# FFN activations turned in squares of 32 on VectorE and carried to their partitions through DRAM, instead of transposes on TensorE

## The chip, the cores and the metric

The kernel runs on one core of a Trainium2 chip. The metric is the device time of one execution in microseconds, the median of several runs. A core has five engines with queues of their own, which meet only at semaphores: TensorE (PE; its weight loads are listed as PEld), VectorE (DVE), ScalarE (ACT), GpSimd (POOL) and SyncE (SP). Here SP issues every DMA. SBUF and PSUM have 128 partitions; TensorE writes to PSUM only.

## The reference, cut to what matters

One layer of a diffusion transformer in float32: modulation, two kinds of attention, an output projection, a LayerNorm, and then the part that the change touches, a SwiGLU FFN with 256 tokens, width 2048 and hidden width 5632:

```python
def swiglu(u, w_gate, w_up, w_down):
    return (jax.nn.silu(u @ w_gate) * (u @ w_up)) @ w_down

x = layer_norm(DN_ALPHA * x + g2 * swiglu(modulate(x, sh2, sc2), w_gate[layer], w_up[layer], w_down[layer]),
               ln2_g[layer], ln2_b[layer])
```

## The kernel before

**Products.** Every float32 product is made of three matmuls. A matrix is split in a high part `hi` (rounded to the TensorE's fp32r type by a ScalarE cast) and a low part `lo` (the rest, a VectorE subtraction); `mm3` (lines 224 to 226) adds x_hi·w_hi, x_hi·w_lo and x_lo·w_hi into one PSUM bank.

**A step.** `load_split` loads 1 MB of a weight, 4 row tiles of 128 by 512 columns, with one DMA on SP (`load_raw`, line 194) into one of 4 `raw` buffers, and splits it in two halves of 128x1024 (`split_raw`, lines 214 and 215) into one of 4 `hi` and 4 `lo` buffers. `project` then runs 24 matmuls on it: 4 row tiles, 2 token tiles `t`, 3 products. So one half serves 12 matmuls, and the four halves in the buffers serve two steps. The order of a queue here is the order in which the tile framework's scheduler puts the instructions; only an earlier part of the kernel has its order written out by hand (`Flow`).

**The FFN.** The hidden width is cut into 11 blocks `f` of 512. For the first 10 blocks, one or two of the four row groups have been multiplied earlier and their sums kept in `spills[f]`, a pair of tiles for gate and up. The main loop over `f` does the remaining groups, first of `w_gate`, then of `w_up`: 3 + 3 steps for blocks 0 to 2, 2 + 2 for blocks 3 to 9, 4 + 4 for block 10. After the last step `activate` adds the kept sums (lines 1291 and 1292), applies silu on ScalarE (line 1295) and multiplies on VectorE (line 1297): `hh`, 128 tokens by 512 hidden columns, for each `t`.

**The flip.** The product with `w_down` sums over the hidden width, so hidden columns have to lie on partitions. `flip` transposes `hh` on TensorE, four transposes of 128x128 against an identity into one PSUM bank (line 1304), and `split` (lines 220 and 221) makes `hTh[f]` and `hTl[f]` of it. Flips wait in the list `flips` and are run after the first step of the next block. `hTh[f+1]` and `hTl[f+1]` lie in the memory of `spills[f]`.

**w_down.** Four column blocks `n` of 512 follow; each takes 11 steps, and step g needs `hTh[g]` and `hTl[g]`. Beside them VectorE sums the rows of the gate g2 from `w_ada` (line 332, 1 MB loads that share the `raw` buffers), and two loads of 1 MB bring ln2's rows. After each column block `residual` (lines 962 to 964) scales, adds and takes statistics; the last LayerNorm ends the kernel.

Of the kernel before, what the change touches and what calls it, by code (L numbers as in the profile page):

```python
# [12 lines left out]
F32 = mybir.dt.float32  # L13
# [4 lines left out]
AF = mybir.ActivationFunctionType  # L18
# [17 lines left out]
NB = 512  # L36
# [113 lines left out]
def dit_layer(ctx: ExitStack, tc: tile.TileContext, x, c, cx, c_ctx, w_ada, b_ada, w_in, q_norm_g,  # L150
              k_norm_g, sink_logit, w_out, ln1_g, ln1_b, w_gate, w_up, w_down, ln2_g, ln2_b,
              rope_cos, rope_sin, out):
    nc = tc.nc
    x, c, cx = x[0], c, cx[0]
# [11 lines left out]
    def wk_bank():  # L166
        return wk_ps.tile([P, NB], F32, tag="wk", name="wk")
# [51 lines left out]
    def split(hi, lo, src):  # L219
        nc.scalar.copy(hi, src)  # L220
        nc.vector.tensor_tensor(lo, src, hi.bitcast(F32), op=ALU.subtract)
# [184 lines left out]
    def t2k(name, shape=(P, NB), dtype=F32):  # L406
        return pa.tile(list(shape), dtype, tag="t2k", name=name, bufs=T2K)
# [551 lines left out]
    def residual(t, n, ps, gate, base, pool, bufs):  # L959
        y = pool.tile([P, NB], F32, tag="t2k", name="yt", bufs=bufs)  # L960
        sl = slice(n * NB, (n + 1) * NB)
        nc.vector.tensor_mul(y, ps, gate[:, sl])
        nc.vector.tensor_add(base[:, t, sl], base[:, t, sl], y)
        nc.vector.bn_stats(stats[:, t, n, :], base[:, t, sl])
# [205 lines left out]
    a = F.add("SP", 1000, ln_loads)  # L1170
    a = F.add("PE", 150, ln_flip, [(a, -SLACK)], [lroom])
# [4 lines left out]
    a = flow_vector((3 * D, 4 * D), NB, adav, (END - 14, END + 24))  # L1176
# [64 lines left out]
    a = F.add("DVE", 3300, lambda: scalars(0), [outs[n, 0] for n in range(4)])  # L1241
# [5 lines left out]
    ea.close()  # L1247


    pb = ctx.enter_context(tc.tile_pool(name="pb", bufs=1, reuse_waits="tile"))  # L1250
    u2h = pb.tile([P, KD, SEQ], F32R, tag="u2h", name="u2h")
    u2l = pb.tile([P, KD, SEQ], F32R, tag="u2l", name="u2l")
    hTh = [pb.tile([P, 4, SEQ], F32R, tag=f"hTh{f}", name="hTh") if f < KF // 4 - SPLIT_F else None for f in range(KF // 4)]
    hTl = [pb.tile([P, 4, SEQ], F32R, tag=f"hTl{f}", name="hTl") if f < KF // 4 - SPLIT_F else None for f in range(KF // 4)]

    def z_part(kk):
        ps = wk_bank()
        for j in range(2):
            for t in range(NT):
                nc.tensor.transpose(ps[:, (j * 2 + t) * P : (j * 2 + t + 1) * P],  # L1260
                                    xt[:, t, (kk + j) * P : (kk + j + 1) * P], ident)
        uf = pb.tile([P, 2, SEQ], F32, tag="t2k", name="uf2", bufs=3)
        for j in range(2):
            nc.scalar.activation(uf[:, j, :], ps[:, j * SEQ : (j + 1) * SEQ], AF.Identity,
                                 bias=mB[:, kk + j : kk + j + 1], scale=mA[:, kk + j : kk + j + 1])
        nc.scalar.copy(u2h[:, kk : kk + 2, :], uf)
        nc.vector.tensor_tensor(u2l[:, kk : kk + 2, :], uf, u2h[:, kk : kk + 2, :].bitcast(F32), op=ALU.subtract)
# [16 lines left out]
            for t in range(NT):  # L1284
                mm3(accs[t], u2h[:, k, t * P : (t + 1) * P], u2l[:, k, t * P : (t + 1) * P], w[j], k == first, k == last)

    def activate(f, t, gate, up, spill):

        if spill is not None:
            sg, su = spill[0][:, t, :], spill[1][:, t, :]  # L1290
            nc.vector.tensor_add(sg, sg, gate)
            nc.vector.tensor_add(su, su, up)
# [4 lines left out]
        nc.vector.tensor_mul(hh, up, sl)
        return hh

    def flip(f, t, hh):  # L1300

        ps = wk_bank()
        for j in range(4):
            nc.tensor.transpose(ps[:, j * P : (j + 1) * P], hh[:, j * P : (j + 1) * P], ident)  # L1304
        if hTh[f] is None:
            hTh[f] = pb.tile([P, 4, SEQ], F32R, tag=f"hTh{f}", name="hTh")
            hTl[f] = pb.tile([P, 4, SEQ], F32R, tag=f"hTl{f}", name="hTl")
        split(hTh[f][:, :, t * P : (t + 1) * P], hTl[f][:, :, t * P : (t + 1) * P], ps.rearrange("p (j q) -> p j q", j=4))

# [3 lines left out]
    spills, first_half = [], []  # L1313
# [18 lines left out]
    def z_rest(t, kk):  # L1332

        ps = zbanks[t, kk]
        tt = slice(t * P, (t + 1) * P)
        uf = pb.tile([P, 2, SEQ], F32, tag="t2k", name="uf2", bufs=3)[:, :, :P]
        for j in range(2):
            nc.scalar.activation(uf[:, j, :], ps[:, j * P : (j + 1) * P], AF.Identity,
                                 bias=mB[:, kk + j : kk + j + 1], scale=mA[:, kk + j : kk + j + 1])
        nc.scalar.copy(u2h[:, kk : kk + 2, tt], uf)  # L1340
        nc.vector.tensor_tensor(u2l[:, kk : kk + 2, tt], uf, u2h[:, kk : kk + 2, tt].bitcast(F32), op=ALU.subtract)  # L1341
# [39 lines left out]
        z_part(kk)  # L1381
    run(first_half[cutoff:])
    flips = []
    for f in range(FFN // NB):
        if 5 <= f < 9:
            residual_base(f - 5)
        gu = []
        for w_ in (w_gate, w_up):
            accs = [acc_bank() for _ in range(NT)]
            g0 = groups[f]  # L1390
            for g in range(g0, ng):
                project(accs, w_, f, g, g0 * 4, KD - 1)
# [3 lines left out]
        for t in range(NT):
            hh = activate(f, t, gu[0][t], gu[1][t], spills[f] if f < SPLIT_F else None)
            flips.append(lambda f=f, t=t, hh=hh: flip(f, t, hh))
    while flips:
        flips.pop(0)()  # L1400
# [97 lines left out]
```

## Time and profile before

| | |
|---|---|
| three runs | 1173.62 us median (1171.78 to 1175.6) |
| the profiled execution | 1172.63 us; span from first to last instruction 1170.9 us |
| mean granted TensorE clock | 0.995 |
| TensorE matmul busy / weight loads | 1144.9 us / 928.6 us |
| VectorE / ScalarE / GpSimd busy | 822.3 / 537.5 / 25.5 us |
| DMA | 292.95 MB, mean 250 GB/s |
| FFN main loop, from block 0's first step to block 10's last | about 611 to 911 us of the span |
| w_down | about 911 to 1150 us |

Times in the views are microseconds from the start of the span. A row of the timeline reads: start, duration, engine, line, operation, out<-in, shape, count, and in brackets how long the engine was idle before and what ended that. A row of the groups reads: line, engine, operation, shapes, count | busy us, mean ns of one | idle time before. Matmuls overlap in the pipeline, so the distance between their starts counts, not their length.

### The profile page before, as it was taken

How to read it: one execution, taken by the hardware profiler on the slowest of the kernel's cores; microseconds unless marked ns; L12 is line 12 of the kernel's file. 1: busy time of each engine (PE TensorE's matmuls, PEld its weight loads, DVE VectorE, ACT ScalarE, POOL GpSimd, SP SyncE). 2: the span in 40 equal slices, each digit the busy share in tenths (PEclk: the TensorE clock that was granted, in tenths of full speed). 3: DMA queues.
4: the chain of work that ended last, by engine and by line, in shares of the span. 5: the costliest groups of instructions: out<-in, count | busy, mean ns of one | idle time of the engine just before them, and what ended most of it. 6: DMA issues, size and time to landing. Idle time of an engine off the chain costs nothing.

```text
span 1170.9 us, 14367 instructions
## 1 busy us (share of the span) xinstructions
PE 1144.9 (98%) x5563; PEld 928.6 (79%) x5563; DVE 822.3 (70%) x1064; ACT 537.5 (46%) x760; POOL 25.5 (2%) x44
## 2 busy tenths in 40 slices
PE   8999999999999989999999999999999999999995
PEld 8767588888887778888888888888888788888884
DVE  4763588888899887766767566665665777676556
ACT  3341542777776255545454444444444433433440
POOL 1000030000000000000000000000000000000000
PEclk9999999999999999999999999999999999999997
DMA  8999988526587678889957555555556898877531
GB/s 266 390 403 397 357 360 287 181 72 215 182 290 280 225 271 320 302 293 316 322 194 239 182 189 196 188 180 180 184 198 212 299 330 317 283 257 256 192 132 73
DMA packets 150716, 292.95 MB, mean 250 GB/s; under 512 B 5580, under 2 KB 20332, under 8 KB 148343
## 3 DMA queue, kind: packets, MB, share of 16 engines
q1 hardware_dynamic: 150648, 292.04, 71.4%
q8 instruction: 44, 0.72, 0.2%
q14 instruction: 24, 0.20, 0.0%
HBM read 289.92 MB, written 2.10 MB: 249 GB/s over the span
## 4 chain that ended last, share of the span: by engine, by line
PE 93%; DVE 4%; DMA 2%; ACT 1%; issue 0%; SPq 0%; DVEq 0%; ACTq 0%
PE acc L224 27%; PE acc L225 27%; PE acc L226 27%; PE wk L865 2%; PE wk L485 2%; PE acc L1070 1%; PE wk L854 1%; PE wk L1304 1%; PE wk L224 1%; PE wk L226 1%; PE wk L225 1%; PE wk L342 1%; DMA lgb<-in_ln_b_dram 1%; PE wk L572 1%; DVE adav L332 1%; DVE lo L215 0%
## 5 line engine op out<-in xcount | busy, mean ns | idle before, releaser
L215 DVE TENSOR_TENSOR lo<-raw,hi 128x1024 fp32r<-128x1024 f32 x258 | 313.8, 1223 | 206.0 <-ACT hi L214 202.6
L214 ACT CAST hi<-raw 128x1024 fp32r<-128x1024 f32 x258 | 271.1, 1055 | 353.0 <-PE acc L226 331.3
L224 PE MATMUL acc<-hi,u2h 128*128 128x512 f32 x704 | 275.5, 391 | 1.2 <-ACT u2h L1340 1.2
L225 PE MATMUL acc<-lo,u2h 128*128 128x512 f32 x704 | 274.2, 389 | 0.8 <-DVE lo L215 0.8
L226 PE MATMUL acc<-hi,u2l 128*128 128x512 f32 x704 | 274.1, 389 | 0.0
L225 PEld LDWEIGHTS acc<-lo,u2h 128*128 128x128 f32 x704 | 132.2, 188 | 28.4 <-DVE lo L215 1.6
L224 PEld LDWEIGHTS acc<-hi,u2h 128*128 128x128 f32 x704 | 132.2, 188 | 28.2 <-ACT u2h L1340 1.4
L226 PEld LDWEIGHTS acc<-hi,u2l 128*128 128x128 f32 x704 | 132.2, 188 | 27.7 <-DVE u2l L1341 0.2
L446 ACT CAST hi<-raw 128x1024 fp32r<-128x1024 f32 (+1 forms) x86 | 87.9, 1033 | 135.3 <-PE acc L226 68.9
L224 PE MATMUL acc<-hi,hTh 128*128 128x512 f32 x344 | 135.5, 394 | 0.0
L226 PE MATMUL acc<-hi,hTl 128*128 128x512 f32 x344 | 134.0, 390 | 0.0
L225 PE MATMUL acc<-lo,hTh 128*128 128x512 f32 x344 | 134.0, 389 | 0.0
L332 DVE SCALAR_TENSOR_TENSOR adav<-raw,cs,adav 128x512 f32<-128x512 f32 (+1 forms) x128 | 121.4, 948 | 9.0 <-DMA raw<-in_w_ada_dram 7.2
L449 DVE TENSOR_TENSOR lo<-raw,hi 128x1024 fp32r<-128x1024 f32 (+1 forms) x86 | 102.5, 1198 | 28.0 <-ACT hi L446 27.7
L224 PE MATMUL acc<-hi,uh 128*128 128x512 f32 x256 | 102.8, 402 | 1.0 <-ACT hi L446 1.0
L225 PE MATMUL acc<-lo,uh 128*128 128x512 f32 x256 | 100.2, 391 | 1.1 <-DVE lo L449 1.1
L226 PE MATMUL acc<-hi,ul 128*128 128x512 f32 x256 | 99.9, 390 | 0.0
L225 PEld LDWEIGHTS acc<-lo,hTh 128*128 128x128 f32 x344 | 64.6, 188 | 14.4 <-issue 1.0
L224 PEld LDWEIGHTS acc<-hi,hTh 128*128 128x128 f32 x344 | 64.6, 188 | 14.1 <-issue 1.0
L226 PEld LDWEIGHTS acc<-hi,hTl 128*128 128x128 f32 x344 | 64.6, 188 | 13.4
L224 PEld LDWEIGHTS acc<-hi,uh 128*128 128x128 f32 x256 | 48.1, 188 | 17.7 <-issue 4.6
L225 PEld LDWEIGHTS acc<-lo,uh 128*128 128x128 f32 x256 | 48.1, 188 | 11.0 <-DVE lo L449 2.0
(201 smaller groups left out, 1166.8 us busy)
## 6 DMA issues: line engine op xcount, KB each, us to landing
raw<-in_w_ada_dram SPq DMA_DIRECT2D x72, 1024.0 KB, 7.0
raw<-in_w_gate_dram SPq DMA_DIRECT2D x44, 1024.0 KB, 5.2
raw<-in_w_up_dram SPq DMA_DIRECT2D x44, 1024.0 KB, 5.1
raw<-in_w_down_dram SPq DMA_DIRECT2D x44, 1024.0 KB, 5.6
raw<-in_w_ada_dram SPq DMA_DIRECT2D x48, 512.0 KB, 4.9
raw<-in_w_in_dram SPq DMA_DIRECT2D x18, 1024.0 KB, 8.0
raw<-in_w_out_dram SPq DMA_DIRECT2D x16, 1024.0 KB, 4.9
raw<-in_w_in_dram SPq DMA_DIRECT2D x10, 512.0 KB, 8.2
```

The costliest lines, as they stand in the source:

```text
L214: nc.scalar.copy(hi[:, :n], raw[:, s : s + n])
L215: nc.vector.tensor_tensor(lo[:, :n], raw[:, s : s + n], hi[:, :n].bitcast(F32), op=ALU.subtract)
L224: nc.tensor.matmul(ps, lhsT=xh, rhs=w[0], start=first, stop=False)
L225: nc.tensor.matmul(ps, lhsT=xh, rhs=w[1], start=False, stop=False)
L226: nc.tensor.matmul(ps, lhsT=xl, rhs=w[0], start=False, stop=last)
L332: nc.vector.scalar_tensor_tensor(a[:, c : c + piece], raw[:, f : f + piece], cs[:, g * (G4 * NB // w) + j, 2:3], a[:, c : c + piece], op0= ...
L342: nc.tensor.matmul(ps, lhsT=ones, rhs=sb[:, s : s + NB], start=True, stop=True)
L446: nc.scalar.copy(hl.hi[:, :n], raw.t[:, s : s + n])
L449: nc.vector.tensor_tensor(hl.lo[:, :n], raw.t[:, s : s + n], hl.hi[:, :n].bitcast(F32), op=ALU.subtract)
L485: nc.tensor.matmul(bank.t[32 * j : 32 * j + 32, :width], lhsT=cs[:, k, 2 - 2 * i : 34 - 2 * i], rhs=raw.t[:, c * width : (c + 1) * width], ...
L572: nc.tensor.transpose(ps.t[:, (j * 2 + t) * P : (j * 2 + t + 1) * P], src, ident)
L865: nc.tensor.matmul(o_ps.t[:, : 2 * P], lhsT=v, rhs=pT.t[:, k].rearrange("p h q -> p (h q)"), start=k == 0, stop=k == 3)
```

## The change

The flip leaves TensorE and PSUM. `activate` writes its product in place (for blocks 0 to 9 in the gate half of the spill, for block 10 in a scratch buffer). `squares` turns each square of 32x32 within `hh` on VectorE, one instruction for a 128x512 tile: what stood on partition i of a group of 32 is now at column i, but the groups of 32 partitions are still in their old place. `put` writes the result to a tile in DRAM, one DMA for each group of 32 partitions, in runs of 128 values (512 B); `get` reads it back with rows of 512 values to the 128 partitions where the hidden columns belong. `place` then splits the SBUF tile into `hTh[f]` and `hTl[f]`, as before from PSUM. For each block that is 2 VectorE transposes, 8 puts of 64 KB and 2 gets of 256 KB, all on SP. The three parts are held back by `turn`, which counts steps: puts after 6 further steps in the order of the program, gets after 8, placing after 9. Two pools of small buffers grow from 3 to 4.

```diff
+PUT, GET, PLACE = 6, 8, 9
...
+    scratch = ctx.enter_context(tc.tile_pool(name="scratch", bufs=1, space=bass.MemoryType.DRAM))
...
-    def activate(f, t, gate, up, spill):
-
-        if spill is not None:
-            sg, su = spill[0][:, t, :], spill[1][:, t, :]
+    def activate(f, t, gate, up, hh):
+
+        if f < SPLIT_F:
+            sg, su = spills[f][0][:, t, :], spills[f][1][:, t, :]
             nc.vector.tensor_add(sg, sg, gate)
             nc.vector.tensor_add(su, su, up)
             gate, up = sg, su
-        sl = pb.tile([P, NB], F32, tag="t2k", name="sl", bufs=3)
-        nc.scalar.activation(sl, gate, AF.Silu)
-        hh = pb.tile([P, NB], F32, tag="t2k", name="hh", bufs=3)
-        nc.vector.tensor_mul(hh, up, sl)
-        return hh
-
-    def flip(f, t, hh):
-
-        ps = wk_bank()
-        for j in range(4):
-            nc.tensor.transpose(ps[:, j * P : (j + 1) * P], hh[:, j * P : (j + 1) * P], ident)
+        nc.scalar.activation(hh, gate, AF.Silu)
+        nc.vector.tensor_mul(hh, up, hh)
...
+    def squares(hh, hx):
+        nc.vector.transpose(hx.rearrange("p (r q i) -> p q r i", r=4, q=Q), hh.rearrange("p (q r i) -> p q r i", r=4, q=Q))
+
+    def put(hx):
+        hd = scratch.tile([4, 32, 4, P], F32, tag="hd", name="hd", bufs=4)
+        for a in range(4):
+            nc.sync.dma_start(hd[:, :, a, :].rearrange("r i x -> i r x"),
+                              hx[32 * a : 32 * a + 32, :].rearrange("i (r x) -> i r x", r=4))
+        return hd
+
+    def get(hd, hf):
+        nc.sync.dma_start(hf, hd.rearrange("r i a x -> (r i) (a x)"))
+
+    def place(f, t, hf):
+
         if hTh[f] is None:
             hTh[f] = pb.tile([P, 4, SEQ], F32R, tag=f"hTh{f}", name="hTh")
             hTl[f] = pb.tile([P, 4, SEQ], F32R, tag=f"hTl{f}", name="hTl")
-        split(hTh[f][:, :, t * P : (t + 1) * P], hTl[f][:, :, t * P : (t + 1) * P], ps.rearrange("p (j q) -> p j q", j=4))
+        hi, lo = (h[f][:, :, t * P : (t + 1) * P].rearrange("p q (a i) -> p q a i", a=4) for h in (hTh, hTl))
+        split(hi, lo, hf.rearrange("p (a q i) -> p q a i", a=4, q=Q))
+
+    def flip_steps(f, gu):
+
+        if f < SPLIT_F:
+            hh, hx = ([c[:, t, :] for t in range(NT)] for c in spills[f])
+        else:
+            hh, hx = ([t2k(name) for t in range(NT)] for name in ("hh", "hx"))
+        for t in range(NT):
+            activate(f, t, gu[0][t], gu[1][t], hh[t])
+            squares(hh[t], hx[t])
...
+        return [[PUT, puts], [GET, gets], [PLACE, places]]
...
+    def turn():
+
+        for e in flips:
+            e[0] -= 1
+        for e in [e for e in flips if e[0] <= 0]:
+            flips.remove(e)
+            e[1]()
+
...
             for g in range(g0, ng):
                 project(accs, w_, f, g, g0 * 4, KD - 1)
-                while flips:
-                    flips.pop(0)()
+                turn()
             gu.append(accs)
...
+        flips += flip_steps(f, gu)
...
             for t in range(NT):
                 mms(g * 4, w, t)
+            turn()
```

On TensorE the order changes only by the transposes that are gone: 8 behind the first step after each of the blocks 0 to 9, and 4 + 4 inside the first step of w_down for block 10. On the other engines the instructions move. (Line numbers of the changed kernel are higher: lo is L216, the cast hi L215, the split of the turned tile L221 and L222, the sums L1293 and L1294.)

VectorE from the gate sums of one of the blocks 3 to 9 to those of the next, before:

```order
L1291 TENSOR_TENSOR spill<-spill,acc 128x512 x2
L215 TENSOR_TENSOR lo<-raw,hi 128x1024 x4
L1292 TENSOR_TENSOR spill<-spill,acc 128x512 x2
L1297 TENSOR_TENSOR hh<-spill,sl 128x512
L215 TENSOR_TENSOR lo<-raw,hi 128x1024
L1297 TENSOR_TENSOR hh<-spill,sl 128x512
L215 TENSOR_TENSOR lo<-raw,hi 128x1024 x2
L221 TENSOR_TENSOR hTl<-wk,hTh 128x4x128 x2
L215 TENSOR_TENSOR lo<-raw,hi 128x1024
```

and now:

```order
L1293 TENSOR_TENSOR spill<-spill,acc 128x512 x2
L216 TENSOR_TENSOR lo<-raw,hi 128x1024 x4
L1294 TENSOR_TENSOR spill<-spill,acc 128x512 x2
L1297 TENSOR_TENSOR spill<-spill 128x512 x2
L1307 STREAM_TRANSPOSE spill<-spill 128x4x4x32 x2
L216 TENSOR_TENSOR lo<-raw,hi 128x1024 x2
L222 TENSOR_TENSOR hTl<-spill,hTh 128x4x128 x2
L216 TENSOR_TENSOR lo<-raw,hi 128x1024 x2
```

Both products and both transposes now stand in one run behind the up sums, with no lo between; the hTl after them belongs to the block before, not to this one.

ScalarE in the same stretch, from the silu of a block on, now:

```order
L1296 ACTIVATE spill<-spill 128x512 x2
L215 CAST hi<-raw 128x1024 x3
L221 CAST hTh<-spill 128x4x128
L215 CAST hi<-raw 128x1024
L221 CAST hTh<-spill 128x4x128
L215 CAST hi<-raw 128x1024 x4
```

The cast of a turned tile (of the block before) used to wait for TensorE; here its input `spill` is what the get has brought, and the fourth hi stands behind it.

SP between the loads of one block (the first gate load stands ahead of these rows), now, with the semaphores that each waits for (DVE, or one of the eight that the DMAs take in turn):

```order
L1312 DMA hd<-spill 32x4x128 [waits DVE_49]
L1312 DMA hd<-spill 32x4x128 x2
L195 DMA raw<-in_w_gate_dram 128x4x512 [waits DMAHW5_49,DVE_49]
L1312 DMA hd<-spill 32x4x128 [waits DMAHW6_49]
L1312 DMA hd<-spill 32x4x128 [waits DMAHW7_49]
L1312 DMA hd<-spill 32x4x128 [waits DMAHW0_49]
L1312 DMA hd<-spill 32x4x128 [waits DMAHW1_49]
L1312 DMA hd<-spill 32x4x128 [waits DMAHW2_49]
L195 DMA raw<-in_w_up_dram 128x4x512 [waits DMAHW3_49,DVE_49]
L195 DMA raw<-in_w_up_dram 128x4x512 [waits DMAHW4_49,DVE_49]
L1317 DMA spill<-hd 128x512 [waits DMAHW6_49,DMAHW5_49]
L1317 DMA spill<-hd 128x512 [waits DMAHW2_49,DMAHW7_49,DMAHW1_49,DMAHW0_49]
```

Before, these were four loads in a row, two of gate and two of up. The first put waits for the squares of the block that ended last. Three puts stand ahead of the second gate load and five behind it; the gets stand behind both up loads and wait for the puts.

More of the change, by code (lines that the diff above doesn't have):

```diff
@@ L1261, in z_part @@
                                     xt[:, t, (kk + j) * P : (kk + j + 1) * P], ident)
-        uf = pb.tile([P, 2, SEQ], F32, tag="t2k", name="uf2", bufs=3)
+        uf = pb.tile([P, 2, SEQ], F32, tag="t2k", name="uf2", bufs=4)
         for j in range(2):
@@ L1293, in activate, with t2k @@
             gate, up = sg, su
-        sl = pb.tile([P, NB], F32, tag="t2k", name="sl", bufs=3)
-        nc.scalar.activation(sl, gate, AF.Silu)
-        hh = pb.tile([P, NB], F32, tag="t2k", name="hh", bufs=3)
-        nc.vector.tensor_mul(hh, up, sl)
-        return hh
-    def flip(f, t, hh):
-        ps = wk_bank()
-        for j in range(4):
-            nc.tensor.transpose(ps[:, j * P : (j + 1) * P], hh[:, j * P : (j + 1) * P], ident)
+        nc.scalar.activation(hh, gate, AF.Silu)
+        nc.vector.tensor_mul(hh, up, hh)
+    Q = 4
+    def t2k(name):
+        return pb.tile([P, NB], F32, tag="t2k", name=name, bufs=4)
+    def squares(hh, hx):
[9 more added lines that the diff above has]
+    def place(f, t, hf):
         if hTh[f] is None:
@@ L1307, in flip, with puts, gets, places @@
             hTl[f] = pb.tile([P, 4, SEQ], F32R, tag=f"hTl{f}", name="hTl")
-        split(hTh[f][:, :, t * P : (t + 1) * P], hTl[f][:, :, t * P : (t + 1) * P], ps.rearrange("p (j q) -> p j q", j=4))
+        hi, lo = (h[f][:, :, t * P : (t + 1) * P].rearrange("p q (a i) -> p q a i", a=4) for h in (hTh, hTl))
[8 more added lines that the diff above has]
+            squares(hh[t], hx[t])
+        hd, hf = {}, {}
+        def puts():
+            for t in range(NT):
+                hd[t] = put(hx[t])
+        def gets():
+            for t in range(NT):
+                hf[t] = hh[t] if f < SPLIT_F else t2k("hf")
+                get(hd[t], hf[t])
+        def places():
+            for t in range(NT):
+                place(f, t, hf[t])
+        return [[PUT, puts], [GET, gets], [PLACE, places]]
     groups = [1 if f < ONE_F else EARLY_G if f < SPLIT_F else 0 for f in range(FFN // NB)]
@@ L1335, in z_rest @@
         tt = slice(t * P, (t + 1) * P)
-        uf = pb.tile([P, 2, SEQ], F32, tag="t2k", name="uf2", bufs=3)[:, :, :P]
+        uf = pb.tile([P, 2, SEQ], F32, tag="t2k", name="uf2", bufs=4)[:, :, :P]
         for j in range(2):
@@ L1392, in dit_layer @@
                 project(accs, w_, f, g, g0 * 4, KD - 1)
-                while flips:
-                    flips.pop(0)()
+                turn()
             gu.append(accs)
[L1396 to L1400, printed above, removed]
+        flips += flip_steps(f, gu)
     l2 = pb.tile([P, 2, D], F32, tag="u2l", name="l2")
@@ L1432, in tail @@
                     mms(g * 4, w, t)
-                residual(t, n, accs[t], g2sb, xt, pb, 3)
+                residual(t, n, accs[t], g2sb, xt, pb, 4)
         return [lambda g=g: step(g) for g in range(KF // G4 - together)] + [tail]
```

## The prediction

> **What bounds the kernel now.** I read the page first: which engine is full, and which the chain of waits runs over.
>
> ```profile
> span 1170.9 us, 14367 instructions
> ...
> PE 1144.9 (98%) x5563; PEld 928.6 (79%) x5563; DVE 822.3 (70%) x1064; ACT 537.5 (46%) x760; POOL 25.5 (2%) x44
> ...
> PE 93%; DVE 4%; DMA 2%; ACT 1%; issue 0%; SPq 0%; DVEq 0%; ACTq 0%
> ...
> raw<-in_w_up_dram SPq DMA_DIRECT2D x44, 1024.0 KB, 5.1
> ```
>
> TensorE sets the end: 93% of the chain. Work taken from it is gained one for one as long as nobody else makes it wait. Next come the windows, for the room elsewhere (us; busy time of PE, PEld, DVE, ACT, POOL; clock, DMA share, GB/s), and the waits.
>
> ```profile
> 5.00:14.00 9.00, 9.00 (x89) 8.68 (x88) 0.00 (x0) 0.57 (x1) 0.00 (x0) 1.00 0.99 310
> ...
> 737.00:895.00 158.00, 158.00 (x724) 131.44 (x723) 98.04 (x106) 72.18 (x83) 0.00 (x0) 1.00 0.57 186
> 915.00:970.00 55.00, 55.00 (x240) 44.83 (x239) 40.90 (x46) 21.68 (x23) 0.96 (x2) 1.00 0.91 328
> ...
> ACT hi L214 <- PE acc L226: 331.3, 211, 3.5
> ...
> SPq L194 <- DVE lo L215: 413.4, 100, 7.2
> ```
>
> From 737 to 895 (FFN blocks 4 to 10) PE never idles, VectorE is busy 62% and the DMA engines 57%. Casts wait for PE to free a hi/lo buffer, and loads wait for VectorE to free a raw buffer: everybody upstream is as far ahead as the buffers let them be. That is the cover for what the change adds.
>
> **What is removed.** The chain in order of time (start, us, what) and PE's timeline give the price of the flips.
>
> ```profile
> 736.43 0.87 PE wk L1304 x8
> 759.09 0.87 PE wk L1304 x8
> ...
> 758.47 0.39 PE L225 MATMUL acc<-lo,u2h 128*128 128x512 f32 x1
> 758.69 0.39 PE L226 MATMUL acc<-hi,u2l 128*128 128x512 f32 x1
> 758.93 1.03 PE L1304 MATMUL wk<-ident,hh 128*128 128x128 f32 x8
> 759.72 0.48 PE L224 MATMUL acc<-hi,u2h 128*128 128x512 f32 x1
> 760.03 0.40 PE L225 MATMUL acc<-lo,u2h 128*128 128x512 f32 x1
> 760.26 0.39 PE L226 MATMUL acc<-hi,u2l 128*128 128x512 f32 x1
> ...
> 911.84 0.39 PE L224 MATMUL acc<-hi,hTh 128*128 128x512 f32 x1
> 912.94 0.66 PE L1304 MATMUL wk<-ident,hh 128*128 128x128 f32 x4 [0.71 <-DVE hh L1297]
> 914.49 0.40 PE L224 MATMUL acc<-hi,hTh 128*128 128x512 f32 x1
> ```
>
> Matmuls start every 0.227 us. From 758.69 to 760.26 three starts take 1.57 instead of 0.68: eight transposes cost 0.89 us. The period says the same: 759.09 - 736.43 = 22.66, less 96 matmuls x 0.227 = 21.77. Ten blocks: 8.9 us. The last block's flips fall between 911.84 and 914.49: three starts take 2.65 instead of 0.68, so 1.97, its 0.71 wait for VectorE included. Removed from PE: **10.9 us**. PE gets nothing in return.
>
> **VectorE and ScalarE.** Groups and timeline:
>
> ```profile
> L221 DVE TENSOR_TENSOR hTl<-wk,hTh 128x512 fp32r<-128x512 f32 x22 | 14.1, 682 | 0.0
> ...
> L588 DVE TENSOR_TENSOR ul<-uf,uh 128x512 fp32r<-128x512 f32 x14 | 9.8, 731 | 5.7 <-ACT uh L585 5.6
> ...
> L585 ACT CAST uh<-uf 128x512 fp32r<-128x512 f32 x14 | 8.3, 641 | 0.1
> ...
> 774.74 1.23 DVE L215 TENSOR_TENSOR lo<-raw,hi 128x1024 fp32r<-128x1024 f32 x1 [1.49 <-ACT hi L214]
> 775.89 1.28 DVE L1292 TENSOR_TENSOR spill<-spill,acc 128x512 f32<-128x512 f32 x2
> 777.08 0.69 DVE L1297 TENSOR_TENSOR hh<-spill,sl 128x512 f32<-128x512 f32 x1
> ...
> 775.91 0.39 PE L226 MATMUL acc<-hi,u2l 128*128 128x512 f32 x1
> ...
> 779.05 1.05 ACT L214 CAST hi<-raw 128x1024 fp32r<-128x1024 f32 x1 [1.14 <-PE acc L226]
> ```
>
> The split of the turned tile now reads SBUF instead of PSUM, and the row of such a split (L588) is 0.05 us longer: nothing, since VectorE is not the bound. New are 22 square transposes, 128x512 f32, which no row shows. All VectorE rows of that size lie near 0.7 us; I take 0.7, from 0.5 (a gain on no path) to 2.0 (three passes). Where they matter: let T be the end of a block's last matmul, which starts at 775.91, so T = 776.1. In the new order (shown with the change) VectorE does the up sums 1.28, both products 1.38 and both transposes 1.4 in one run, where a lo stood between the products before. It starts some 0.2 after T, is free at T+4.2, and the next lo is ready at T+5.4. Four lo stand between gate sums and up sums, and of the four hi/lo buffers only the one of the last half step is still in use at T. So three halves lie ready for PE, 12 matmuls or 2.72 us each, and PE needs the next lo at T+8.2. That covers the run by 2.8 us. With no halves in store the whole run would stand on PE's path, and the 1.4 of the transposes would cost 15 us over 11 blocks.
>
> The skill gives a price of its own: in the Trainium skill, VectorE: DVE Perf Modes, "The three transpose paths", 128x128 bf16 takes 311 ns on VectorE; four of them would be an estimated 1.2 us, and the sum would stay the same. No run so far shows it.
>
> **SP and the DMA trip.** SP's timeline (start, us from first to last issue):
>
> ```profile
> 773.28 6.02 SPq L194 DMA_DIRECT2D raw<-in_w_gate_dram  x2
> 784.11 6.71 SPq L194 DMA_DIRECT2D raw<-in_w_up_dram  x2
> ...
> out_dram<-xt SPq DMA_DIRECT2D x8, 256.0 KB, 2.3
> ...
> raw<-in_w_ada_dram SPq DMA_DIRECT2D x2, 1024.0 KB, 7.9
> ```
>
> Against T = 776.1 the loads leave at -2.8, +2.8, +8.0 and +14.3. The pair of gate loads belongs to the next block but one, and SP takes its queue in order. Now three puts stand ahead of the second load and wait for the squares: they leave at T+4.2, the load at T+5.4 (2.6 late), five puts by T+7.5, and the up loads behind them on time. Per block SP issues ten more, about 0.4 us each: 4 of 21.8. A raw tile is cast three steps of 5.44 us after its issue, so 2.6 late plus 5.1 of landing is covered. The gets stand behind the second up load: T+14.7. Each put takes a semaphore of eight in turn, so the eighth waits until the first has landed. With a landing of L for a put and G for a get, the data are there at T + max(14.7, 4.2 + 2L) + G. ScalarE has that cast behind the third hi after the next block's gate sums; it can make this hi when the last step's first half frees its buffer, so it reaches the cast at T+21.8-2.7+1.1 = T+20.1. The hi behind it feeds the lo due at T+29.9 (a period of 21.77 after T+8.16), so PE notices only data later than T+27.0: 29.9 less lo 1.22, hi 1.05 and the cast itself 0.64. L and G are bounded by 2.3 (the 256 KB stores) and 7.9 (megabytes in pieces of 512 B, queued in pairs, the two ada loads above). I take 5.1, as behind one weight load: there at T+19.8, no wait. At 7.9: T+27.9, 0.9 a block. Traffic: 5 MB a block for 4 raises the share from 0.57 to 0.74 in the shorter period; pieces of 512 B ran at 310 GB/s with 0.99 busy, so they are about as cheap per byte as the 326 (186/0.57) of this stage; if each cost as much as a 2 KB piece, 1280 beside 2048, the share would be 0.96. Cost: nothing, up to 9 us.
>
> **First column block of w_down.** Block 10's puts and gets fall here, and its two splits come between gate-2 sums; the two loads of ln2 move out to later blocks.
>
> ```profile
> 972.29 0.69 DVE L962 TENSOR_TENSOR yt<-acc,g2sb 128x512 f32<-128x512 f32 x1 [1.31 <-PE acc L226]
> ...
> 978.80 1.22 DVE L215 TENSOR_TENSOR lo<-raw,hi 128x1024 fp32r<-128x1024 f32 x1
> ...
> 980.48 0.39 PE L225 MATMUL acc<-lo,hTh 128*128 128x512 f32 x1
> ...
> 901.41 5.51 DMA raw<-in_w_ada_dram
> ```
>
> VectorE has 14 us idle in the window 915:970 for 1.4 us of transposes, and DMA exchanges 2 MB of ln2 for 1 MB. But the lead is thin at the end: a lo done at 980.02 is used at 980.48. It follows the last matmuls, not the sums, so it should stay; VectorE idles 1.31 us ahead of it. I count 0, up to 5 us (an ada load held back behind the gets).
>
> **Sum.** Profiled execution 1172.63 (span 1170.9 plus 1.7 around it) - 10.9 + 0 = 1161.7. The median of the runs is 0.99 above that execution: 1162.7.
>
> **Rivals.**
> (1) The gain shrinks in the first w_down block: gets wait for puts on SP, ada loads stand behind them, and a VectorE sum waits in order with the lo behind it. For: the chain at 901.41 crosses just such a load for 5.51 us; the share there is 0.91. Against: ln2 is gone from there. Loss 2.5 to 5 (a landing of 5.1, less a lead of up to 2.7): 1165 to 1168.
> (2) The trip through DRAM is late in every block. ScalarE waits at the cast in order, with the next hi behind it. It decides from L = G = 7.6; each us of L then costs 3 us in ten blocks. Break-even is 8.0 (1.1 x 10): no change, 1173. At 9.0 it costs 4.2 a block: 1162.7 + 42 = **1205, slower**. For: eight issues chained by a semaphore, writes to DRAM in pieces that no row shows. Against: the 2.3 us stores.
> The Trainium skill speaks for this one: VectorE: DVE Perf Modes, "The three transpose paths" and "Rules for kernel authors", keeps TensorE for a 128x128 transpose and calls a strided plain copy far slower than the crossbar where the innermost step is large. Here both sides move whole runs of 128 values, so its condition is not met; no run here shows such a copy.
> (3) The transposes are slow: from 2.1 us each VectorE is late for the next lo. At 3.0 it is 1.9 a block, 11 blocks: 1162.7 + 21 = 1184. Against: every row of that size is near 0.7.
>
> **Chances.** Forecast (1160 to 1165) 0.73; (1) 0.13; (2) near break-even 0.05; (2) beyond it 0.06; (3) 0.03. A measurement of this kernel tells about 0.3%, 3.5 us, from no change: faster 0.86, same 0.05, slower 0.09. The likeliest is 1162.7; the range is 1159.5 (the runs scatter by 2) to 1168.5, which takes in rival (1).
>
> **What would show it.** Right: no L1304 row; a period near 21.8 between equal sums of blocks 4 to 9; PE idle nowhere new from 640 to 900; transposes under 2 us; gets landed before their casts, so no wait of hTh for a DMA. Wrong: PE waiting for lo behind hTl or hTh (2), behind a transpose (3), or around the first w_down block (1); DMA share above 0.9 in the FFN blocks.

## The result and the profile after

The changed kernel takes 1164.81 us (median of 4 runs, 1161.41 to 1164.91), the kernel before 1172.98 beside it: a ratio of 0.9919, 95% interval 0.9903 to 0.9936. Faster, by 8.2 us or 0.8%; the forecast was 1162.7, from 1159.5 to 1168.5. The profiled execution took 1164.91 us. The page of the changed kernel:

```profile
span 1163.1 us, 14314 instructions
...
PE 1138.2 (98%) x5475; PEld 922.3 (79%) x5475; DVE 833.6 (72%) x1086; ACT 537.6 (46%) x760; POOL 23.5 (2%) x44
...
PE 95%; DVE 3%; DMA 1%; ACT 1%; issue 0%; SPq 0%; DVEq 0%; ACTq 0%
```

TensorE has 88 instructions fewer, which are the 88 transposes of 11 blocks, and is still 95% of the chain. The span is 7.7 us shorter (1170.85 and 1163.13 to the hundredth). Where does that come from? Three points of TensorE's timeline divide the program: block 0's first product with a lo half, w_down's first, and the end of the span. First the kernel before, then the changed one:

```profile
608.69 0.39 PE L225 MATMUL acc<-lo,u2h 128*128 128x512 f32 x1
911.39 0.39 PE L225 MATMUL acc<-lo,hTh 128*128 128x512 f32 x1
```

```profile
611.85 0.39 PE L226 MATMUL acc<-lo,u2h 128*128 128x512 f32 x1
905.61 0.39 PE L226 MATMUL acc<-lo,hTh 128*128 128x512 f32 x1
```

| us | before | changed | difference |
|---|---|---|---|
| start to block 0 (same instructions in both) | 608.69 | 611.85 | +3.16 |
| blocks 0 to 10 | 302.70 | 293.76 | -8.94 |
| w_down to the end | 259.46 | 257.52 | -1.94 |
| span | 1170.85 | 1163.13 | -7.72 |

So there are two stories. In the part that was changed the gain is 10.88 us, against 10.9 forecast. And ahead of it, where every engine has the same instructions in the same order as before (only a pool of small buffers is larger), this execution lost 3.16. The windows of the changed kernel show where (us; busy time of PE, PEld, DVE, ACT, POOL with counts; clock, DMA share, GB/s):

```profile
415.90:419.31 3.41, 1.18 (x8) 1.08 (x9) 3.38 (x7) 0.73 (x2) 0.00 (x0) 1.00 0.20 74
419.31:422.73 3.42, 3.42 (x10) 2.64 (x9) 3.38 (x8) 2.57 (x7) 0.00 (x0) 0.50 0.58 184
129.18:132.59 3.41, 3.41 (x9) 2.65 (x10) 2.51 (x3) 1.88 (x3) 0.00 (x0) 0.50 1.03 398
```

From 129.18 and from 419.31, for 3.41 us each, TensorE's clock was granted at 0.50. Matmuls start every 0.43 us there (419.69, 420.12, 420.54) instead of every 0.23, so 8 fit where 15 would; the counts in the rows, 9 and 10, take in those that reach over an edge. Each such stretch costs some 1.6 us, and two of them make up the 3.16. Both come right behind a gap in TensorE's work. The kernel before has the same gaps and, in its profiled execution, no such stretch. Runs e7 to e10 take this up.

In the FFN blocks everything stands as forecast. The window of the changed kernel that answers to the one shown of before:

```profile
737.00:895.00 158.00, 158.00 (x699) 130.83 (x698) 109.78 (x125) 75.50 (x86) 0.00 (x0) 1.00 0.74 243
```

Its group of the square transposes of blocks 0 to 9:

```profile
L1307 DVE STREAM_TRANSPOSE spill<-spill 128x512 f32<-128x512 f32 x20 | 13.0, 686 | 0.0
```

ScalarE's waits from 640 to 900 us, the one row of the turned tiles (total, times, longest):

```profile
ACT hTh L221 <- DMA spill<-hd: 0.5, 1, 0.5
```

The DMA issues of puts and gets there (KB each, median us to landing):

```profile
hd<-spill SPq DMA_DIRECT2D x80, 64.0 KB, 4.2
spill<-hd SPq DMA_DIRECT2D x20, 256.0 KB, 5.3
```

TensorE never idles, the DMA share is 0.74, a square transpose takes 0.69 us, and ScalarE waits for a turned tile once, for 0.5 us. The steps around the end of a block (T = 753.2, the end of its last matmul), on VectorE, TensorE, and, one block later (T = 775.0), on SP and ScalarE:

```profile
752.81 1.28 DVE L1294 TENSOR_TENSOR spill<-spill,acc 128x512 f32<-128x512 f32 x2
...
755.21 1.29 DVE L1307 STREAM_TRANSPOSE spill<-spill 128x512 f32<-128x512 f32 x2
756.43 1.18 DVE L216 TENSOR_TENSOR lo<-raw,hi 128x1024 fp32r<-128x1024 f32 x1
...
753.28 0.39 PE L226 MATMUL acc<-lo,u2h 128*128 128x512 f32 x1
761.45 0.39 PE L226 MATMUL acc<-lo,u2h 128*128 128x512 f32 x1
775.04 0.39 PE L226 MATMUL acc<-lo,u2h 128*128 128x512 f32 x1
...
777.70 1.29 SPq L1312 DMA_DIRECT2D hd<-spill  x3
779.40 0.40 SPq L195 DMA_DIRECT2D raw<-in_w_gate_dram  x1
779.84 2.64 SPq L1312 DMA_DIRECT2D hd<-spill  x5
782.88 5.75 SPq L195 DMA_DIRECT2D raw<-in_w_up_dram  x2
788.72 0.97 SPq L1317 DMA_DIRECT2D spill<-hd  x2
...
795.06 0.61 ACT L221 CAST hTh<-spill 128x512 fp32r<-128x512 f32 x1
```

The period is 775.04 - 753.28 = 21.76. The lo behind the transposes is done at 757.6 and used at 761.45: a lead of 3.8 us. The gets leave at T+13.7 and T+14.2, the data are there 5.3 later, at T+19.0 and T+19.5, and ScalarE comes to the first cast at T+20.1.

### The profile page after: what moved, and what is told of

It is laid out like the page before. It is cut to its first block, busy times and chain, and to the rows that moved or that the text cites. A ratio compares the mean times of both kernels' runs of the same rounds, so it can differ in the third digit from the quotient of the medians.

```text
span 1163.1 us, 14314 instructions
## 1 busy us (share of the span) xinstructions
PE 1138.2 (98%) x5475; PEld 922.3 (79%) x5475; DVE 833.6 (72%) x1086; ACT 537.6 (46%) x760; POOL 23.5 (2%) x44
## 4 chain that ended last, share of the span: by engine, by line
PE 95%; DVE 3%; DMA 1%; ACT 1%; issue 0%; SPq 0%; DVEq 0%; ACTq 0%
PE acc L225 28%; PE acc L226 28%; PE acc L227 27%; PE wk L866 2%; PE wk L486 2%; PE acc L1071 1%; PE wk L855 1%; PE wk L225 1%; PE wk L227 1%; PE wk L226 1%; PE wk L343 1%; PE wk L573 1%; DMA lgb<-in_ln_b_dram 1%; DVE xt L1495 0%; PE wk L919 0%; DVE xt L1496 0%
## 5 line engine op out<-in xcount | busy, mean ns | idle before, releaser
L216 DVE TENSOR_TENSOR lo<-raw,hi 128x1024 fp32r<-128x1024 f32 x258 | 312.3, 1221 | 186.5 <-ACT hi L215 183.3
L215 ACT CAST hi<-raw 128x1024 fp32r<-128x1024 f32 x258 | 270.9, 1055 | 342.2 <-PE acc L227 310.0
L225 PE MATMUL acc<-hi,u2h 128*128 128x512 f32 x704 | 275.3, 391 | 1.2 <-ACT u2h L1383 1.2
L225 PEld LDWEIGHTS acc<-hi,u2h 128*128 128x128 f32 x704 | 132.5, 188 | 28.8 <-ACT u2h L1383 1.4
L225 PE MATMUL acc<-hi,hTh 128*128 128x512 f32 x344 | 135.5, 394 | 0.0
L225 PE MATMUL acc<-hi,uh 128*128 128x512 f32 x256 | 103.3, 404 | 1.0 <-ACT hi L447 1.0
L225 PEld LDWEIGHTS acc<-hi,hTh 128*128 128x128 f32 x344 | 64.6, 188 | 14.3 <-issue 0.7
L225 PEld LDWEIGHTS acc<-hi,uh 128*128 128x128 f32 x256 | 48.5, 190 | 17.9 <-ACT hi L447 4.4
```

Of the source, the lines that this page charges most:

```text
L215: nc.scalar.copy(hi[:, :n], raw[:, s : s + n])
L216: nc.vector.tensor_tensor(lo[:, :n], raw[:, s : s + n], hi[:, :n].bitcast(F32), op=ALU.subtract)
L225: nc.tensor.matmul(ps, lhsT=xh, rhs=w[0], start=first, stop=False)
```

## The experiments

The theory is that the gain is TensorE's own time, one for one, because VectorE's run and the trip through DRAM stay within their covers; what is lost against it is the clock. The rivals are those of the prediction (the trip late, the transposes slow, w_down's first block), and that the change costs something everywhere which the removed flips outweigh. All runs are read by three lengths that the clock ahead of block 0 does not touch: blocks 0 to 10, w_down to the end, and both together, the FFN stretch.

| run | us, profiled | us, median | half-clock stretches ahead of the end | blocks 0 to 10 | w_down on | FFN stretch |
|---|---|---|---|---|---|---|
| before | 1172.63 | 1172.98 | 0 | 302.70 | 259.5 | 562.2 |
| changed | 1164.91 | 1164.81 | 2 | 293.76 | 257.5 | 551.3 |
| e1 no turn, no trip | 1162.77 | 1162.78 | 1 | 293.76 | 257.4 | 551.1 |
| e2 squares x3 | 1161.84 | 1164.63 | 0 | 293.76 | 257.5 | 551.3 |
| e3 squares x5 | 1168.25 | 1167.69 | 1 | 299.26 | 257.9 | 557.1 |
| e4 block 10 on TensorE | 1163.34 | 1164.78 | 0 | 293.76 | 259.5 | 553.2 |
| e5 second trip | 1190.65 | 1189.86 | 6 | 309.1 | 271.0 | 580.1 |
| e6 gets early | 1162.34 | 1161.74 | 1 | 293.76 | 257.5 | 551.3 |
| e7 junk in gaps | 1162.01 | 1162.01 | 0 | 293.76 | 257.5 | 551.3 |
| e8 changed again | 1163.25 | 1163.80 | 1 | 293.76 | 257.6 | 551.3 |
| e9 before with junk | 1172.88 | 1172.64 | 0 | 302.69 | 259.8 | 562.5 |
| e10 junk again | 1161.64 | 1161.70 | 0 | 293.76 | 257.5 | 551.3 |

The part ahead of block 0, which the three lengths leave out, goes by the half-clock stretches that lie in it, whichever kernel it is. Block 0's first product with a lo half starts at 608.3 to 608.9 us in the seven profiles without one (before, e2, e4, e5, e7, e9, e10; the six of e5 come later), at 609.2 to 610.2 in the four with one (e1, e3, e6, e8), and at 611.85 in the changed kernel with two. Three of the seven (e2, e4, e5) are variants of the changed kernel without the junk matmuls of e7, so the change itself costs nothing there that can be measured.

**e1: without turn and trip.**

```diff
-            squares(hh[t], hx[t])
...
-        return [[PUT, puts], [GET, gets], [PLACE, places]]
+        hf = {t: hh[t] for t in range(NT)}
+        return [[PLACE, places]]
```

> The changed kernel without the squares, the puts and the gets; the product hh is split as it lies, unturned, so the FFN's output is another one. TensorE's order is that of the changed kernel. FFN stretch = from block 0's first product with a lo half to the end of the span: 562.2 us before (1170.9 - 608.7), 551.25 after (1163.1 - 611.85). Theory (the additions are covered, the gain is TensorE's own time): 551.2 within 0.5, so nothing is left to gain by making turn and trip free. Rivals (the additions cost something that the removed flips outweighed): shorter than 551 by what they cost, several us. The part ahead of 608 is the same code in all; in the profile of the changed kernel it took 3.2 us longer than before, in two stretches of 3.4 us at half clock. If these come and go by the run, this run's time is 1161.4, 1163.1 or 1164.8 by their number (0, 1, 2).

Measured: blocks 0 to 10 take 293.76, the same to a hundredth, and the stretch is 551.1. VectorE's transposes, 80 puts and 20 gets of the FFN blocks cost TensorE nothing that can be measured; the two rivals with a hidden price fall. The profiled execution is 2.1 shorter than that of the changed kernel, while the FFN stretch is 0.2 shorter: the rest lies ahead of block 0 (609.78 against 611.85), where it has one stretch of half clock less.

**e2 and e3: the transposes three and five times.**

```diff
-        nc.vector.transpose(hx.rearrange("p (r q i) -> p q r i", r=4, q=Q), hh.rearrange("p (q r i) -> p q r i", r=4, q=Q))
+        for _ in range(3):
+            nc.vector.transpose(hx.rearrange("p (r q i) -> p q r i", r=4, q=Q), hh.rearrange("p (q r i) -> p q r i", r=4, q=Q))
```

(and `range(5)` for e3.)

> Each square transpose three times: 2.75 us more on VectorE behind the products of each block. In the changed kernel the smallest lead of a lo half behind the transposes was 3.83 us in blocks 3 to 9. Theory: still covered, the lead falls to about 1.1, the period stays 21.77 and the FFN stretch 551.3 within 1. Rival (VectorE is at its limit, or the prediction's cover of 2.8 behind the transposes was the true one and is nearly used up): 0 to 2.7 us a block, the stretch up to 580.

> Each square transpose five times: 5.5 us more on VectorE in one run behind the products of each block. Theory: this passes the lead of 3.83, so TensorE waits 1.7 us for a lo in each of blocks 3 to 9 (period 23.4), somewhat less or nothing in blocks 0 to 2 with their six steps; the stretch grows by 10 to 20, to 561 to 571, and the time to about 1172 to 1184. Rival (the store of halves is deeper or VectorE runs ahead further when pressed): stretch unchanged at 551.

e2 is as expected: the period stays, and the lead falls from 3.8 to 1.46. Rows of e2's timeline (the first of the three lo is done 1.18 us after its start, at 756.86):

```profile
755.68 3.46 DVE L216 TENSOR_TENSOR lo<-raw,hi 128x1024 fp32r<-128x1024 f32 x3
...
758.32 0.39 PE L226 MATMUL acc<-lo,u2h 128*128 128x512 f32 x1
```

In e1, without transposes, it was 5.02. So each transpose takes (5.02 - 3.83)/2 = 0.60 and (3.83 - 1.46)/4 = 0.59 us of it: in a run they follow each other at 0.6, though one alone lasts 0.69. e3 passes the end of the cover, but by less than expected: period 22.18, 0.42 more, where I had 1.7; the stretch, 557.1, and the median, 1167.69, lie below the 561 to 571 and 1172 to 1184 that I expected. Rows of e3's timeline, VectorE's run first, then TensorE at the late half of that block and of the next:

```profile
755.16 6.04 DVE L1308 STREAM_TRANSPOSE spill<-spill 128x512 f32<-128x512 f32 x10
...
761.17 1.07 PE L225 MATMUL acc<-hi,u2h 128*128 128x512 f32 x4
762.36 0.50 PE L226 MATMUL acc<-lo,u2h 128*128 128x512 f32 x1
...
784.54 0.50 PE L226 MATMUL acc<-lo,u2h 128*128 128x512 f32 x1
```

Four more transposes at 0.6 bring the lead from 1.46 to -0.95. But in this kernel the scheduler has put three more of the half's products with hi ahead of the first with lo (four L225 in a row): 0.68 us of work in place of a wait. 0.95 less that is 0.3, near the measured 0.42; where the other 0.1 goes is not shown. Blocks 1, 2 and 10 grow by 0.8 to 0.9 each. The cover ends where the leads say, between three and five transposes; my 1.7 had used 0.69 for each transpose and no such reordering.

**e4: block 10 alone back on TensorE.**

```diff
+        if f == SPLIT_F:
+            hh = [t2k("hh") for t in range(NT)]
+            for t in range(NT):
+                activate(f, t, gu[0][t], gu[1][t], hh[t])
+            return [[1, lambda t=t: flip(f, t, hh[t])] for t in range(NT)]
```

(`flip` is that of the kernel before; it runs ahead of w_down.)

> Block 10 alone goes back to the transposes on TensorE, 4 + 4 inside w_down's first step; its turn and its trip are gone. Theory: the last block's share of the gain is 1.97 (1.26 of matmul starts and 0.71 of waiting for hh), so the FFN stretch is 553.2 (551.25 + 2.0), and the other 8.9 stay. Rival (what is saved in the last block comes from the leads in w_down's first column block, or ln2's loads that moved): 551.3 or less, or over 555.

Measured: 553.2, with 293.76 for the blocks and 259.5 for the rest. On TensorE:

```profile
902.50 0.39 PE L225 MATMUL acc<-hi,hTh 128*128 128x512 f32 x1
903.47 0.66 PE L1331 MATMUL wk<-ident,hh 128*128 128x128 f32 x4 [0.58 <-DVE hh L1297]
...
904.87 0.40 PE L225 MATMUL acc<-hi,hTh 128*128 128x512 f32 x1
```

From 902.50 to 904.87 three starts (there are two between, at 903.88 and 904.55) take 2.37 instead of 0.68, 1.7 of loss, a third of it the wait for VectorE's product (0.58; 0.71 before). The two terms of the sum are thus separate: 8.9 for ten blocks, 1.7 to 2 for the last.

**e5: the trip through DRAM twice.**

```diff
                 get(hd[t], hf[t])
+            for t in range(NT):
+                h2 = scratch.tile([P, NB], F32, tag="h2", name="h2", bufs=4)
+                nc.gpsimd.dma_start(h2, hf[t])
+                nc.gpsimd.dma_start(hf[t], h2)
```

> Behind each get the tile goes through DRAM once more, one DMA out and one back of 256 KB, issued by GpSimd, so that SP's queue is not held; the result is the same. In the changed kernel ScalarE reaches the first cast of a turned tile at 795.06 and needs the data by 802 at the latest before TensorE notices: the hi behind it has 1.1 us of idle ahead of it, VectorE comes to its lo 2.1 later, and that lo leads by 3.83, in all 7.0 (the prediction said T+27.0, which is 801.6 for T = 774.6). The data are there at about 794.5 now; a put of 3 to 4 and a get of 5.3 more bring them at 803 to 805. Theory: TensorE waits 1 to 3 us for a lo in each of blocks 3 to 9: period 22.8 to 24.8, FFN stretch 558 to 572 (551.25 without), run 1168 to 1186. Rival (the trip has far more room than the prediction's T+27): no change, 551.3. Rival (the trip was on the edge already): the whole 8 to 10 us a block, stretch 610 or more.

This is rival 2 made real: 1189.86 us, ratio 1.0137 (1.0112 to 1.0162). ScalarE's group of the cast, from 640 to 900 us (busy, mean, then its idle time ahead of it):

```profile
L221 ACT CAST hTh<-spill 128x512 fp32r<-128x512 f32 x18 | 11.1, 618 | 70.2 <-DMA spill<-h 70.2
```

The timeline of ScalarE and TensorE around two of these casts, and TensorE in w_down:

```profile
763.69 0.62 ACT L221 CAST hTh<-spill 128x512 fp32r<-128x512 f32 x1 [7.85 <-DMA spill<-h]
...
766.57 0.50 PE L226 MATMUL acc<-lo,u2h 128*128 128x512 f32 x1 [0.71 <-DVE lo L216]
...
788.43 0.62 ACT L221 CAST hTh<-spill 128x512 fp32r<-128x512 f32 x1 [9.81 <-DMA spill<-h]
...
790.04 0.50 PE L225 MATMUL acc<-hi,u2h 128*128 128x512 f32 x1 [1.64 <-ACT hi L215]
791.30 0.80 PE L226 MATMUL acc<-lo,u2h 128*128 128x512 f32 x1 [0.76 <-DVE lo L216]
...
972.86 1.22 PE L225 MATMUL acc<-hi,hTh 128*128 128x512 f32 x2 [6.14 <-ACT hi L215]
```

A wait of ScalarE of 7.85 us reaches TensorE as 0.71, one of 9.81 as 1.64 + 0.76: 7.1 and 7.4 us of them are covered, and the rest comes through. The cast at 763.69 stands 33.4 us behind the end of its block (730.3) and costs a period of 22.78, 1.0 more. By this block, TensorE notices casts later than T+32.4. The prediction had T+27.0; but in this kernel the scheduler put the casts two hi further back in ScalarE's queue, five behind the gate sums instead of three, which is 2 x 2.72 = 5.4 us: 27.0 + 5.4 = 32.4. The periods of blocks 3 to 9 are 23.00, 21.76, 22.78, 26.09, 21.79, 25.78 and 21.83, so the expected 22.8 to 24.8 is right on average (23.3), not block by block. The stretch of 580.1 lies above the 558 to 572 expected, and the run above the 1168 to 1186, for two reasons that I had not counted: w_down's part lost 13.5 of its own, with one wait of 6.14 us behind block 10's tiles, and some waits of TensorE are followed by a stretch of half clock. Two windows of this run, the first with the wait of 1.64 ahead of 790, the second with the wait of 0.76:

```profile
787.40:790.80 3.40, 1.51 (x6) 0.69 (x4) 1.47 (x2) 2.37 (x4) 0.00 (x0) 1.00 0.03 12
790.80:794.20 3.40, 2.90 (x7) 2.32 (x8) 3.40 (x6) 2.19 (x3) 0.00 (x0) 0.50 0.47 118
```

Five such places, one of them of double length, make six stretches of half clock, of up to 1.6 each.

**e6: the gets early in SP's queue.** The edit is `PUT, GET, PLACE = 1, 1, 1` for `6, 8, 9`.

> Puts, gets and placing are called with PUT, GET, PLACE = 1, 1, 1, which puts the two gets of a block around its second weight load in SP's queue, where they stand and wait until the puts have landed; the casts stand one hi earlier or so in ScalarE's queue. The second load leaves some 5 us later than in the changed kernel, the two loads behind it some 4 later. Theory: a load that is 2.6 late plus 5.3 of landing used half of the 16.3 of its cover; 5 more still fit: period 21.77, stretch 551.3 within 0.5, while ScalarE's waits for a DMA rise from 0.5 us to some us a block. Rival (SP's queue is what decides, and the place of the gets is why the change is free): TensorE waits in every block, the stretch grows by 10 or more.

TensorE is as expected: 293.76 and 551.3. But my reason was wrong: next to nothing waited. From 640 to 900 us SP's gets waited for puts 2.5 us in all, 0.3 at the longest, and ScalarE for no DMA. SP's timeline behind the end of a block (T = 772.4) and the first cast:

```profile
775.11 3.73 SPq L1312 DMA_DIRECT2D hd<-spill  x8
779.00 0.34 SPq L1317 DMA_DIRECT2D spill<-hd  x1
779.39 0.43 SPq L195 DMA_DIRECT2D raw<-in_w_gate_dram  x1
...
780.61 5.41 SPq L195 DMA_DIRECT2D raw<-in_w_up_dram  x2
...
784.25 0.62 ACT L221 CAST hTh<-spill 128x512 fp32r<-128x512 f32 x1
```

The DMA issues from 640 to 900 us:

```profile
hd<-spill SPq DMA_DIRECT2D x80, 64.0 KB, 1.7
spill<-hd SPq DMA_DIRECT2D x20, 256.0 KB, 3.9
```

With no weight load between them, a put lands in 1.7 us (median) instead of 4.2, so the first get leaves right behind the eighth put, at T+6.6 instead of T+13.7. The second weight load leaves at T+7.0, 2.6 later than in the changed kernel and not 5, the up loads 0.3 later and not 4, and the cast at T+11.9 waits for nothing. Whether gets that really stand in SP's queue for long would hurt was not shown by this run.

**e7, e8: junk in the gaps, and the change again.**

```diff
         nc.tensor.transpose(lroom.t[:, : 2 * KD], lrow, ident[: 2 * KD, : 2 * KD])
+        warm(lroom.t[:, P : 2 * P], 5)
...
     first_products(0, 0)
+    for _ in range(10):
+        nc.tensor.matmul(firsts[1][1], u2h[:, 0, :P], first_gate[0][0].hi[:, :NB], start=True, stop=True)
```

> The changed kernel with matmuls of no use in the two gaps of TensorE where its clock fell: 5 of 128x128 behind the transpose of lrow (line 1168, gap of 0.96 and 0.76 us around 128), 10 of 128x512 into a bank not yet in use behind the first products (gap of 2.73 around 417). In the six profiles so far, TensorE's clock was granted at half for one stretch of 3.413 us right after a stretch of that grid in which PE was busy 0.50 or less (0.34, 0.36, 0.50, 0.50), and never after one of 0.56 or more; where the grid falls differs by run. With the gaps filled no stretch of the grid falls below 0.6. Theory (the steps of 1.7 us between runs of one kernel are these stretches): no record of half clock ahead of the kernel's end, every run near 1161.4, none near 1163.1 or 1164.8, and a median about 2 to 3 below the changed kernel's. Rival (the stretches come from elsewhere): the same mixture of 1161.4 to 1164.8 as the changed kernel.

> The changed kernel once more, beside the one with the filled gaps. Theory: runs near 1161.4, 1163.1 and 1164.8, by 0, 1 or 2 stretches at half clock, median 1163 to 1165; FFN stretch 551.25 as in the first profile, whatever the run's time. Rival: one narrow group of times, or a stretch that differs from profile to profile.

e7: five runs from 1161.27 to 1162.31, median 1162.01, ratio to the kernel before 0.9899 (0.9884 to 0.9914). e8, on the same chip: six runs, 1160.98, 1161.09, 1163.25, 1164.34, 1164.55 and 1165.91, median 1163.80, ratio 0.9911 (0.9892 to 0.9931). The mixture is gone where the gaps are filled. The two intervals overlap; what carries the reading is the spread, 1.0 against 4.9, the granted clock (0.995 and 0.996 in the runs of e7; in e8 0.995 in the two runs at 1161, down to 0.992 in the one at 1165.91) and the traces. First two windows of e8, the stretch with the gap and the one behind it:

```profile
413.63:417.04 3.41, 0.65 (x6) 0.56 (x6) 3.33 (x8) 0.08 (x1) 0.00 (x0) 1.00 0.36 138
417.04:420.45 3.41, 3.41 (x10) 2.67 (x10) 3.35 (x7) 3.22 (x8) 0.00 (x0) 0.50 0.44 110
```

TensorE's timeline of e8 there:

```profile
416.51 0.63 PE L1234 MATMUL wk<-ident,xt 128*128 128x128 f32 x4 [2.76 <-DVE xt L987]
```

And the window at that place in e7:

```profile
415.50:418.90 3.40, 2.90 (x16) 2.17 (x15) 3.33 (x7) 1.51 (x5) 0.00 (x0) 1.00 0.01 1
```

The gap of 2.76 us leaves 0.65 us of work in a stretch of 3.41, and the next stretch is granted 0.50. In e7 the junk fills that place, and the clock stays 1.00. One expectation was off in its detail: the lowest e8 runs lie 0.3 to 0.4 under the 1161.4 named, and the highest lies 1.1 above the 1164.8 named for two stretches; no trace of it was kept.

**e9, e10: both kernels with junk.** e9 is the kernel before with the edit of e7; e10 is e7 once more.

> The kernel before with the same junk matmuls in the two gaps, so that both kernels can be compared without the stretches of half clock. Theory (gain of 10.95 from TensorE's time, the rest of the measured difference is the clock): no stretch of half clock ahead of the end, runs in a narrow group at about 1172.3, and the changed kernel with junk 10.0 to 11.0 us below in the median. Rival (the change itself gives some of its gain back in a way that the one profile does not show): a difference of 8 to 9, as between the two kernels without junk.

> The changed kernel with junk once more, on the same chip as the kernel before with junk. Theory: 1161.2 to 1162.4 in every run, 10.0 to 11.0 below its partner. Rival: runs at 1163 and above come back, so that the narrow group of the first time was luck.

Measured: 1172.64 (11 runs, 1171.78 to 1173.14) and 1161.70 (4 runs, 1161.34 to 1162.16). The difference is 10.94 us; the gain of the changed part in the first two profiles was 10.88. The runs of the plain kernel before, beside them, went up to 1175.48. So the 2 to 3 us that the first result lacked are the clock's, and the change gives nothing back. The changed kernel with junk, the fastest in the median together with e6, has a ratio of 0.9902 (0.9887 to 0.9917).

## Why the prediction was right, point by point

- **Removed, 8.9 + 1.97.** Blocks 0 to 10 are 8.94 shorter, the period went from 22.65 to 21.76, and w_down on is 1.94 shorter; e4 brings back 1.9 of that. The reading of "three starts take 1.57 instead of 0.68" holds, and e9 and e10 give the sum as 10.94.
- **VectorE.** Taken 0.7 for a transpose, measured 0.69, and 0.6 each in a run. The cover was forecast as 2.8 and is 3.8. The need at T+8.2 was exact (761.45); the lo is ready at T+4.4, not T+5.4, because the up sums start 0.4 ahead of T instead of 0.2 behind it, and two transposes take 1.2 instead of 1.4. The 0.2 behind T was misread: the prediction's own row has the sums start at 775.89, 0.2 ahead of its T = 776.1. Rival 3 would have needed about 2.5 us a transpose, not 2.1. The estimate from the Trainium skill, VectorE: DVE Perf Modes, "The three transpose paths" (four times 311 ns, 1.2 us), does not agree with 0.69: here the whole 128x512 tile is one instruction, at the pace of any other of its size.
- **The trip.** The puts leave at T+2.7 (forecast 4.2: the first tile does not wait for the second), the second gate load at T+4.4 (5.4), the puts are through at T+7.5 (7.5), the gets leave at T+13.7 (14.7). Landings of 4.2 and 5.3, taken as 5.1 both; the data at T+19.0 to 19.5 (19.8), the cast at T+20.1 (20.1), DMA share 0.74 (0.74). That TensorE notices only past T+27.0 was tested by e5 in another order of casts; the one block worked out there fits once the two hi are counted that the scheduler moved.
- **w_down's first block, count 0.** ScalarE's waits for w_down's loads do grow (total, times, longest), here before and then after, where 13.1 of the 17.4 us fall in the first block:

```profile
ACT hi L214 <- DMA raw<-in_w_down_dram: 8.7, 2, 4.8
```

```profile
ACT hi L215 <- DMA raw<-in_w_down_dram: 17.4, 5, 5.3
```

Without the trip (e1) they are 8.5, so the growth comes with the trip. VectorE and TensorE of the changed kernel at the thinnest place of that block:

```profile
952.79 2.36 DVE L216 TENSOR_TENSOR lo<-raw,hi 128x1024 fp32r<-128x1024 f32 x2 [0.25 <-ACT hi L215]
...
955.47 0.39 PE L226 MATMUL acc<-lo,hTh 128*128 128x512 f32 x1
```

That is near rival 1's mechanism (a late DMA reaches TensorE through a lo), but the leads take it: the thinnest lo there is done at 954.0 (952.79 + 1.22) and used at 955.47, a lead of 1.5 us; before it was 2.2. The thin lead that the prediction names, 0.46 us at 980.48, belongs to the second step of the next column block, and is 0.7 at the same place now. e1, with no trip at all, takes 257.4 for w_down on, 0.2 less.
- **The sum.** 1161.7 for an undisturbed execution is what e7 and e10 measure for the changed kernel (1162.0 and 1161.7). What failed is the last step, from there to the median: I added 0.99 as the offset of the kernel before, and in a bound took its scatter as "the runs scatter by 2". The scatter is mostly not noise around a time but whole stretches of half clock at some 1.6 each (what is left where the gaps are filled is about 1 us), and three of the changed kernel's first four runs had two of them: one by its trace, the other two by their times and their granted clock, 0.993 in all three against 0.995 in the fourth. So the 0.99 was no fixed offset, but stood for something that comes and goes by the run. The forecast missed the median by 2.1, on the side that the range allowed for rival 1, which did not happen: that the median lies within the range is to that extent luck.
- **Rivals 2 and 3** did not come. e5 shows that rival 2 would have looked as described (ScalarE held at the cast, TensorE behind it for hi and lo, slower than before).

Why the kernel before meets the half clock less often than the changed one, with the same instructions up to 600 us, stays open: 7 of 10 runs of the changed kernel were above 1163, and 13 of 37 of the kernel before above 1173.3. Such a count may be chance, since where the grid of the stretches falls in a gap differs from run to run.

## What to carry to other kernels

Where TensorE sets the end, a transpose on it costs its starts (0.11 us for each 128x128 here), and a detour of some 18 us over VectorE and DRAM is free, as here, as long as each of its steps ends ahead of the first reader that TensorE waits for; count that lead in us for each queue, and count what the scheduler will reorder. When a result misses a sum that every stage of the trace confirms, compare the stages that were not changed, with their granted clock, before inventing a cost for the change. A gap in TensorE's work that is nobody's bottleneck can be worth a few matmuls of no use.

## What was not expected of the hardware

- **The half clock lies on a grid of 3.413 us.** In all twelve profiles a stretch at 0.50 starts a whole number of 3.413 us behind the first clock record. Ahead of the last products it followed every stretch in which PE was busy for 0.50 of the time or less (0.00, 0.19, 0.34, 0.36, 0.39, 0.45, 0.46, 0.48, 0.49, 0.50 and 0.50), and none of 0.55 or more, but for the second half of the double one in e5. At the very end of two runs a stretch of 0.43 was not followed by one, so PE's busy time is near to what counts and not quite it. A gap of 2.7 us was enough when most of it fell within one stretch; split over two (0.63 and 0.57 in the kernel before) it did nothing. The Trainium skill, TensorE: Matmul & The Clock Gate, "Part 1: The HAM clock gate", has a free-running window of 3413 ns, which agrees. By its idle window of about 3.4 us only the stretch of 0.00 in e5 would count among these eleven; the ten with work in them did too, and a gap of 2.7 us was enough.
- **A wait of TensorE can cost a second time** where it empties about half of such a stretch: in e5 the wait of 1.64 us ahead of 790 leaves 1.51 of 3.40 busy, and a stretch at 0.50 follows, which costs up to 1.6.
- **How soon a small transfer lands differed with its neighbours in the queue.** The same 64 KB puts took 4.2 us with a 1 MB load among them (the changed kernel) and 1.7 where they stood together (e6); the 256 KB gets 5.3 behind two loads and 3.9 between them.
- **A 128x512 float32 square transpose on VectorE** lasts 0.69 us, 0.60 from start to start.
